# Turning feed-forward and residual blocks with VectorE block transposes and DRAM transfers

## The chip, the cores and the metric

The kernel runs on one core of one Trainium2 chip. The core has TensorE (PE in the profile; PEld are its weight loads), VectorE (DVE), ScalarE (ACT), GpSimd (POOL) and SyncE (SP), each with its own queue of instructions that run in order, a memory of 128 partitions that all engines read and write (SBUF), an accumulator memory that TensorE writes (PSUM), and DRAM, reached by transfers that SP, ACT or POOL issue. The metric is device microseconds for one execution; less is better. The time before is 2910.77 us, the median of three runs (2910.56 to 2910.94).

## The reference

Two decoder layers over 256 tokens of width 2048, and a last RMSNorm. Each layer runs a mixer (layer 0: HGRN2 and gated DeltaNet heads; layer 1: a Mamba-2 SSD mixer), a cross-attention into 256 memory tokens, and a SwiGLU feed-forward of width 5632, each behind an RMSNorm and added to the residual stream.

```python
for layer in range(DEPTH):
    u = rmsnorm(h, norm_mix[layer])
    mix = hgrn2_gdn_mixer(u, ...) if layer % 2 == 0 else mamba2_mixer(u, ...)
    h = h + mix
    xa = memory_cross_attention(rmsnorm(h, norm_xattn[layer]), rmsnorm(mem, norm_mem[layer]), ...)
    h = h + xa
    hn = rmsnorm(h, norm_ffn[layer])
    h = h + jnp.matmul(jax.nn.silu(jnp.matmul(hn, w_gate[layer])) * jnp.matmul(hn, w_up[layer]), w_down[layer])
return rmsnorm(h, norm_final)
```

All of it is in float32.

## The kernel before

**The matmuls.** All 256 tokens stay on the chip; weights are streamed from DRAM once, in tiles of 128 x 1024 floats (512 KB), four in flight (tag `wr`). A float32 weight is made into two parts of reduced width: ScalarE casts it to a high part `wh`, VectorE subtracts to get the low part `wl` (`split`, L155 to L157; four buffers each). Activations are kept in the same two parts, as operands `u` of 128 features x 4 x 256 tokens (`utiles`, L211). `xstat` (L193) computes 256 tokens x 512 columns: for each 128 rows of the weight, and for each half of the tokens, three matmuls (high by high, high by low, low by high) of 128x128 by 128x512 into a PSUM tile `acc`. So a product with 2048 rows is 16 x 2 x 3 = 96 matmuls. In it the activations are the stationary operand, so they must lie with features on the partitions.

**Where turning is needed.** `xstat` leaves tokens on the partitions. What it gives must be turned, features to the partitions, before it can be an operand again. `turned` (L282) does that on TensorE: eight transposes of 128x128 (through a matmul with the identity) for one block of 256 tokens x 512 features, into two PSUM tiles `mx`, from which ScalarE and VectorE make the two parts of the operand.

**The feed-forward** (`ffn`, L869) runs over 11 blocks of 512 hidden features in groups of 4, 4 and 3. For a block it computes the gate product, applies SiLU on ScalarE into one of the tiles `gate`, `raw` and `w`, then the up product, multiplied in by VectorE. The block is turned (`turn`, L875) one block late, behind the next block's gate product; the last block of a group is turned at the group's end. The turned blocks of a group (`hid`) are then the operand of the group's share of the down projection (`project`, L338), which adds to the residual stream `h`, four tiles `h0` to `h3` of 2 x 128 tokens x 512 features.

**The residual blocks.** A norm that follows the residual stream is a `RowNorm` (L294). As soon as a block `h[nb]` of the stream is complete, `RowNorm.block` (L304) turns it, multiplies it by the norm's gain (ScalarE makes the high part, L312; VectorE the low part, L313) and puts it on the list `u` of operands; `squares` gathers the row sums on ScalarE. There are five such norms: N1 and N2 behind the hybrid mixer and the first cross-attention, N3 behind the first feed-forward, N4 behind the SSD mixer, N5 behind the second cross-attention. N3's operands are wanted first by the SSD stage, whose first product are the step sizes (`wstat`, L172: 32 matmuls of 128x256, over all 16 rows of 128 features), and by B and C; N4's by the query projection of the second cross-attention.

**Order.** The program is written stage by stage; a planner that reckons with its own costs orders the instructions of each engine, allocates the buffers of each tag and adds the semaphores. A helper's line stands for all its uses: L121 is every matmul, L289 every transpose by `turned`, L124 and L127 VectorE's two-operand operations, L156 ScalarE's copies in `split`.

**Tags that the change uses.** `X` and `cv` (one buffer each) and `tmp` (two buffers), 4 KB per partition. Elsewhere they hold, among others, the SSD mixer's x and y of a head group (`cv`, `X`), broadcast decays (`tmp`), the queries and keys of the cross-attention (`cv`, `X`) and, in the last feed-forward's end, early parts of the down projection's weights (L357). POOL issues few transfers before the change: some scratch and row transfers of the mixers and the memory tokens.

Of the kernel before, what the change touches and what calls it, by code (L numbers as in the profile page):

```python
# [9 lines left out]
F32 = mybir.dt.float32  # L10
# [3 lines left out]
AF = mybir.ActivationFunctionType  # L14
ALU = mybir.AluOpType
# [3 lines left out]
P = 128  # L19
# [59 lines left out]
def trunk(ctx: ExitStack, tc: tile.TileContext, A: dict, out: bass.AP):  # L79
    nc = tc.nc  # L80
    pe, act, dve, pool = nc.tensor, nc.scalar, nc.vector, nc.gpsimd
# [5 lines left out]
    dp = ctx.enter_context(tc.tile_pool(name="d", bufs=1, space=bass.MemoryType.DRAM))  # L87
# [28 lines left out]
    def col(name, i=0, n=1):  # L116
        o = COLS[name][0] + i
        return cols[:, o:o + n]
# [4 lines left out]
    def tt(e, o, a, b, op):  # L123
        e.tensor_tensor(o, a, b, op=op)  # L124

    def stt(o, a, s, b, op0, op1):
        dve.scalar_tensor_tensor(o, a, s, b, op0=op0, op1=op1)  # L127

    def t4(tag, shape, dt=F32):
        return mp.tile(shape, dt, name=tag, tag=tag, bufs=BUFS.get(tag, 1))  # L130

    def psb(shape=None):
        return pm.tile(shape or [P, 512], F32, name="mx", tag="mx")
# [21 lines left out]
    def split(hi, lo, src):  # L155
        act.copy(hi, src)  # L156
        tt(dve, lo, src, hi.bitcast(F32), ALU.subtract)  # L157
# [31 lines left out]
    def later_in_stream(ins, n):  # L189

        waiting.append((len(stream) + n - 1, ins))

    def xstat(W, n0, n, u, *rows):  # L193

        accs = [pa.tile([P, n], F32, name="acc", tag="acc") for _ in range(2)]
        rows = rows or ((0, KT),)
        nk = sum(r[1] for r in rows)
        tiles = (t[1:] for r in rows for t in wtiles(W, *r, n0, n))
        for k, (wh, wl) in enumerate(tiles):
            for a in range(2):  # L200
                xh = u[k // 4][0][:, k % 4, a * P:(a + 1) * P]
                xl = u[k // 4][1][:, k % 4, a * P:(a + 1) * P]
                mm(accs[a], xh, wh, k == 0, False)
                mm(accs[a], xh, wl, False, False)
                stream.append(mm(accs[a], xl, wh, False, k == nk - 1))
                for at, ins in waiting:
                    if at == len(stream) - 1:
                        behind(ins, stream[-1])
        return accs

    def utiles():  # L211
        return (up.tile([P, 4, T], F32R, name="u", tag="u"), up.tile([P, 4, T], F32R, name="u", tag="u"))
# [41 lines left out]
    class Norm:  # L254
# [9 lines left out]
        def block(self, nb):  # L264
            src = self.load(nb)
            hi, lo = utiles()
            for c in range(4):
                g = col(self.gain[0], self.gain[1] + nb * 4 + c)
                act.activation(hi[:, c], src[:, c], AF.Copy, scale=g)
                stt(lo[:, c], src[:, c], g, hi[:, c].bitcast(F32), ALU.mult, ALU.subtract)  # L270
            self.u.append((hi, lo))
# [8 lines left out]
    h = [cp.tile([P, 2, 512], F32, name=f"h{nb}") for nb in range(4)]  # L280

    def turned(src, i, ps=None, late=0):  # L282

        if ps is None:
            ps = psb([P, 2, T])
        for x in range(2):
            c = 2 * i + x
            for a in range(2):
                ins = pe.transpose(ps[:, x, a * P:(a + 1) * P], src[a][:, c * P:(c + 1) * P], ident)  # L289
                if late:  # L290
                    later_in_stream(ins, late)
        return ps

    class RowNorm:  # L294


# [4 lines left out]
            self.ss = cp.tile([P, 2, 4], F32, name="rss", tag="rss", bufs=2)  # L301
            self.r = None

        def block(self, nb, src, late=0):  # L304
            op = utiles()
            hi, lo = op
            for i in range(2):
                ps = turned((src[:, 0], src[:, 1]), i, None, late)
                for x in range(2):
                    c = 2 * i + x  # L310
                    g = col(self.gain[0], self.gain[1] + nb * 4 + c)
                    act.activation(hi[:, c], ps[:, x], AF.Copy, scale=g)  # L312
                    stt(lo[:, c], ps[:, x], g, hi[:, c].bitcast(F32), ALU.mult, ALU.subtract)  # L313
            self.u.append(op)
            self.squares(nb, src)
# [22 lines left out]
    def project(W, u, rows, done=None, parts=None):  # L338
        for nb in range(3 if parts else 4):
            for a, acc in enumerate(xstat(W, nb * 512, 512, u, *rows)):  # L340
                hb = h[nb][:, a]
                tt(dve, hb, hb, acc, ALU.add)
                if parts:
                    parts(nb, a, 0, 512)
            if done:
                done(nb)

    def project_by_token(W, u, k0, nk, parts, done):


        t = FIRST[W[0], k0, 3 * 512, 512]
        w = []
        for i in range(nk // 2):
            raw = wp.tile([P, 2, 512], F32, name="wr", tag="wr", bufs=4)
            nc.sync.dma_start(raw, A[W[0]][W[1], t + i].rearrange("p (k n) -> p k n", n=512))
            if i < 2:
                wh, wl = (t4(tag, [P, 2, 512], F32R) for tag in (("X", "cv"), ("tmp", "tmp"))[i])  # L357
            else:
                wh, wl = (wp.tile([P, 2, 512], F32R, name=tag, tag=tag) for tag in ("wh", "wl"))
            split(wh, wl, raw)  # L360
            w.append((wh, wl))
        for a, c, n in ((0, 0, 512), (1, 0, 256), (1, 256, 256)):
            acc = pa.tile([P, n], F32, name="acc", tag="acc")
            for k in range(nk):
                wh, wl = (x[:, k % 2, c:c + n] for x in w[k // 2])
                xh, xl = (x[:, k % 4, a * P:(a + 1) * P] for x in u[k // 4])
                mm(acc, xh, wh, k == 0, False)
                mm(acc, xh, wl, False, False)
                mm(acc, xl, wh, False, k == nk - 1)
            hb = h[3][:, a, c:c + n]  # L370
            tt(dve, hb, hb, acc, ALU.add)
            parts(3, a, c, n)
            if c + n == 512:
                done(a)
# [99 lines left out]
    turns = []  # L474
# [394 lines left out]
    def ffn(layer, N, done=None, parts=None, by_token=None):  # L869
        b0 = 0  # L870
        for nblk in (4, 4, 3):
            hid = []
            late = None

            def turn(sg):  # L875
                hi, lo = op = utiles()
                for i in range(2):
                    split(hi[:, 2 * i:2 * i + 2], lo[:, 2 * i:2 * i + 2], turned(sg, i))
                hid.append(op)

            for b in range(b0, b0 + nblk):
                ga = xstat(("ffn_w_gate", layer), 512 * b, 512, N.u)
                r = N.column()
                sg = t4(("gate", "raw", "w")[b % 3], [P, 2, 512])
                sg = (sg[:, 0], sg[:, 1])
                for a in range(2):
                    act.activation(sg[a], ga[a], AF.Silu, scale=r[:, a:a + 1])
                if late:
                    turn(late)
                ua = xstat(("ffn_w_up", layer), 512 * b, 512, N.u)  # L890
                for a in range(2):
                    stt(sg[a], ua[a], r[:, a:a + 1], sg[a], ALU.mult, ALU.mult)
                late = sg
            turn(late)
            last = b0 + nblk == 11
            project(("ffn_w_down", layer), hid, ((4 * b0, 4 * nblk),), done if last else None, parts if last else None)
            if last and by_token:
                project_by_token(("ffn_w_down", layer), hid, 4 * b0, 4 * nblk, parts, by_token)
            b0 += nblk


    def ssd(N, nxt):
# [93 lines left out]
        r = ssa.column(2 * D)  # L996
        for nb in range(4):
            accs = xstat(Wo, nb * 512, 512, ys, (KT, KT))
            for a in range(2):
                p, hb = part[nb][:, a], h[nb][:, a]  # L1000
                tt(dve, p, p, accs[a], ALU.add)
                stt(hb, p, r[:, a:a + 1], hb, ALU.mult, ALU.add)
            nxt.block(nb, h[nb])


    def load_x(nb):
# [24 lines left out]
    N2 = RowNorm(("norm_ffn", 0))  # L1031
    xattn(0, N1, N2, keys)
    N3 = RowNorm(("norm_mix", 16))
    ffn(0, N2, lambda nb: N3.block(nb, h[nb]))
    N4 = RowNorm(("norm_xattn", 16))
    ssd(N3, N4)
    N5 = RowNorm(("norm_ffn", 16))
    xattn(1, N4, N5)
# [6 lines left out]
    r = cp.tile([P, 2], F32, name="r", tag="r", bufs=2)  # L1045
# [8 lines left out]
    def store(a):  # L1054
# [6 lines left out]
        for nb in range(4):  # L1061
# [5 lines left out]
            nc.sync.dma_start(out[a * P:(a + 1) * P, nb * 512:(nb + 1) * 512], hb)  # L1067

    ffn(1, N5, None, final, store)


# [49 lines left out]
```

## Time and profile before

| | us |
|---|---|
| median of the three runs | 2910.77 |
| the profiled execution | 2911.57 |
| its span, first to last instruction | 2909.8 |
| TensorE busy in it | 2891.2 |
| VectorE busy | 1770.2 |
| ScalarE busy | 1457.6 |
| GpSimd busy | 28.9 |

The granted TensorE clock is 0.998 of full speed over the span. Transfers move 542.36 MB, a mean of 186 GB/s. A busy time counts an instruction from its start to its modelled end; matmuls overlap in TensorE's pipeline, so that the sum of their durations exceeds the time that they take. What ends the program is read from the chain of work: the profile follows the last instruction back to what released it, or to the instruction before it on its engine, and gives each piece its time up to the next.

### The profile page before, as it was taken

What the parts mean: (1) busy time and instruction counts of PE and PEld (TensorE: products, weight loads), DVE (VectorE), ACT (ScalarE), POOL (GpSimd) and SP (SyncE); (2) the same over time, 40 slices, a digit from 0 to 9 for tenths busy, and PEclk for the clock granted to TensorE, in tenths of its full rate; (3) what the DMA queues carried; (4) which work ended last, traced back from release to release, by engine and by line L of the source; (5) the groups of instructions that cost most, each with busy time, mean ns of one, the idle gap of its engine ahead of it and who ended that gap; (6) DMA issues with size and microseconds to landing.
All of it is one profiled execution on the core that took longest, in us unless ns stands there. A gap on an engine that the chain in (4) does not pass through costs nothing.

```text
span 2909.8 us, 35776 instructions
## 1 busy us (share of the span) xinstructions
PE 2891.2 (99%) x13656; PEld 2402.2 (83%) x13656; DVE 1770.2 (61%) x2287; ACT 1457.6 (50%) x1834; POOL 28.9 (1%) x61
## 2 busy tenths in 40 slices
PE   8999999999999999999999999999999999999998
PEld 7888888888888888888888888888888888888887
DVE  6676768865555445445677846787664454455455
ACT  7455547655443443444655645565564443443444
POOL 0000000000000000000000000000000000000000
PEclk9999999999999999999999999999999999999999
DMA  8554544545555555555655555545555555555554
GB/s 284 173 175 141 182 145 164 191 159 188 188 188 195 188 189 192 192 189 187 206 180 195 188 198 186 188 167 182 204 185 190 189 189 194 191 190 191 195 188 153
DMA packets 154749, 542.36 MB, mean 186 GB/s; under 512 B 16968, under 2 KB 23248, under 8 KB 154576
## 3 DMA queue, kind: packets, MB, share of 16 engines
q1 hardware_dynamic: 149872, 525.11, 52.2%
q0 software_dynamic: 4288, 14.69, 1.6%
q8 instruction: 107, 1.75, 0.2%
q14 instruction: 66, 0.54, 0.1%
q10 hardware_dynamic: 416, 0.27, 0.0%
HBM read 536.13 MB, written 3.87 MB: 186 GB/s over the span
## 4 chain that ended last, share of the span: by engine, by line
PE 98%; DVE 1%; ACT 1%; issue 0%; DMA 0%; SPq 0%; DVEq 0%
PE acc L121 91%; PE mx L121 4%; PE mx L289 1%; PE tn L289 1%; PE mx L952 0%; DMA wr<-in_hy_w_in 0%; DVE wl L124 0%; ACT wh L156 0%; DVE tmp L124 0%; PE mx L489 0%; DVE b L127 0%; PE mx L601 0%; DVE X L127 0%; DVE D L124 0%; ACT D L448 0%
## 5 line engine op out<-in xcount | busy, mean ns | idle before, releaser
L121 PE MATMUL acc<-wh,u 128*128 128x512 f32 x7808 | 2445.8, 393 | 7.2 <-ACT wh L156 7.2
L124 DVE TENSOR_TENSOR wl<-wr,wh 128x1024 fp32r<-128x1024 f32 x974 | 1191.3, 1224 | 979.3 <-ACT wh L156 975.9
L121 PEld LDWEIGHTS acc<-wh,u 128*128 128x128 f32 x7808 | 1465.0, 188 | 306.3 <-ACT wh L156 7.2
L156 ACT CAST wh<-wr 128x1024 fp32r<-128x1024 f32 x978 | 1025.6, 1050 | 1210.6 <-PE acc L121 1145.1
L121 PE MATMUL acc<-wl,u 128*128 128x512 f32 x3904 | 1530.8, 392 | 1.3 <-DVE wl L124 1.3
L121 PEld LDWEIGHTS acc<-wl,u 128*128 128x128 f32 x3904 | 735.2, 188 | 151.7 <-DVE wl L124 2.7
L127 DVE SCALAR_TENSOR_TENSOR cv<-tn,cols,cv 128x255 f32<-128x255 f32 (+2 forms) x120 | 57.6, 480 | 19.3 <-ACT cv L395 17.3
L124 DVE TENSOR_TENSOR h<-h,acc 128x512 f32<-128x512 f32 (+1 forms) x89 | 57.6, 675 | 10.5 <-PE acc L121 10.3
L403 ACT ACTIVATE raw<-acc,r 128x512 f32<-128x512 f32 x64 | 42.2, 684 | 23.7 <-PE tn L289 12.0
L127 DVE SCALAR_TENSOR_TENSOR u<-mx,cols,u 128x256 fp32r<-128x256 f32 x96 | 43.2, 479 | 10.4 <-ACT u L312 6.8
L312 ACT ACTIVATE u<-mx,cols 128x256 fp32r<-128x256 f32 x80 | 34.8, 469 | 20.5 <-PE mx L289 18.1
L289 PE MATMUL tn<-cst,raw 128*128 128x128 f32 x272 | 43.7, 272 | 1.0 <-ACT raw L403 1.0
L289 PEld LDWEIGHTS tn<-cst,raw 128*128 128x128 f32 x272 | 34.1, 139 | 10.2 <-ACT raw L403 1.4
L124 DVE TENSOR_TENSOR u<-mx,u 128x512 fp32r<-128x512 f32 x48 | 31.0, 684 | 12.2 <-ACT u L156 12.2
L156 ACT CAST u<-mx 128x512 fp32r<-128x512 f32 x48 | 26.0, 591 | 16.1 <-PE mx L289 10.7
L319 ACT ACTIVATE b<-h 128x512 f32<-128x512 f32 x48 | 29.9, 624 | 1.4 <-DVE h L127 1.4
L121 PEld LDWEIGHTS mx<-tmp 128*127 128x127 f32 (+7 forms) x240 | 24.8, 178 | 1.3 <-issue 0.7
L289 PE MATMUL mx<-cst,h 128*128 128x128 f32 x160 | 25.3, 272 | 0.0
L121 PE MATMUL mx<-tmp 128*127 128x64 f32 (+7 forms) x240 | 25.0, 260 | 0.0
L127 DVE SCALAR_TENSOR_TENSOR kq<-tn,cols,kq 128x255 f32<-128x255 f32 (+2 forms) x48 | 22.8, 475 | 2.4 <-ACT kq L395 2.0
L289 PEld LDWEIGHTS mx<-cst,h 128*128 128x128 f32 x160 | 20.0, 140 | 4.9
L395 ACT ACTIVATE cv<-tn,cols 128x256 f32<-128x256 f32 x40 | 18.6, 466 | 5.2 <-PE tn L289 3.9
(281 smaller groups left out, 1129.0 us busy)
## 6 DMA issues: line engine op xcount, KB each, us to landing
wr<-in_ffn_w_gate SPq DMA_DIRECT2D x176, 512.0 KB, 3.2
wr<-in_ffn_w_up SPq DMA_DIRECT2D x176, 512.0 KB, 3.2
wr<-in_ffn_w_down SPq DMA_DIRECT2D x176, 512.0 KB, 3.2
wr<-in_ssd_w_in SPq DMA_DIRECT2D x161, 512.0 KB, 3.3
wr<-in_hy_w_in SPq DMA_DIRECT2D x129, 512.0 KB, 3.3
wr<-in_ssd_w_out SPq DMA_DIRECT2D x64, 512.0 KB, 3.3
wr<-in_hy_w_out SPq DMA_DIRECT2D x32, 512.0 KB, 4.1
tmp<-rows POOLq DMA_DIRECT2D x18, 512.0 KB, 4.1
```

What stands on the lines that cost most here:

```text
L121: return pe.matmul(o, lhsT=lhsT, rhs=rhs, start=start, stop=stop, skip_group_check=True)
L124: e.tensor_tensor(o, a, b, op=op)
L127: dve.scalar_tensor_tensor(o, a, s, b, op0=op0, op1=op1)
L156: act.copy(hi, src)
L289: ins = pe.transpose(ps[:, x, a * P:(a + 1) * P], src[a][:, c * P:(c + 1) * P], ident)
L312: act.activation(hi[:, c], ps[:, x], AF.Copy, scale=g)
L319: act.activation(t4("b2", [P, 512]), src[:, a], AF.Square, accum_out=self.ss[:, a, nb:nb + 1])
L395: act.activation(c, x, AF.Copy, scale=w[:, 3:4])
L403: act.activation(o[a], accs[a], func, scale=r[:, a:a + 1])
```

## The change

Of the blocks that are turned, some take another way. `turned_by_dma` takes the two token halves of a block (128 tokens x 512 features each). VectorE transposes each in blocks of 32x32 into a tile `y`, so that within each group of 32 partitions features and tokens have changed places. Four transfers, one for each group of 32 partitions, write `y` to a DRAM tile `turns` (two buffers), and one transfer reads it back into a tile `z` in which all 128 partitions are features. POOL issues all five. ScalarE and VectorE then make the operand's two parts from `z` in place of PSUM.

In the feed-forward (both layers) every block takes this way but the last of a group, whose operand is wanted at once. Of the residual blocks, the first three behind the first feed-forward (N3) and the first three behind the SSD mixer (N4) take it; N1, N2, N5 and each fourth block stay with TensorE. `y` and `z` lie in `X` and `cv`, or both in `tmp`, in turn. In a residual block the low part is made in eight operations of 128x128 in place of four of 128x256.

```diff
+    def turned_by_dma(src, tags):
+        y = t4(tags[0], [P, 4, 4, 2, 32])
+        z = t4(tags[1], [P, 4, 8, 32])
+        for a in range(2):
+            dve.transpose(y[:, :, :, a, :].rearrange("p b k c -> p k b c"), src[a])
+        d = dp.tile([4, 32, 4, 256], F32, name="turns", tag="turns", bufs=2)
+        for q in range(4):
+            nc.gpsimd.dma_start(d[:, :, q].rearrange("b r x -> r b x"),
+                                y[32 * q:32 * q + 32].rearrange("r b k a c -> r b (k a c)"))
+        nc.gpsimd.dma_start(z.rearrange("p q k c -> p (q k c)"), d.rearrange("b r q x -> (b r) (q x)"))
+        return z.rearrange("p q k c -> p k q c")
+
+    AWAY = (("X", "cv"), ("tmp", "tmp"))
...
-        def block(self, nb, src, late=0):
+        def block(self, nb, src, late=0, tags=None):
             op = utiles()
             hi, lo = op
-            for i in range(2):
+            if tags:
+                z = turned_by_dma((src[:, 0], src[:, 1]), tags)
+                by32 = lambda x: x.rearrange("p (a q c) -> p a q c", a=2, q=4)
+                for c in range(4):
+                    g, x = col(self.gain[0], self.gain[1] + nb * 4 + c), z[:, 2 * c:2 * c + 2]
+                    act.activation(by32(hi[:, c]), x, AF.Copy, scale=g)
+                    for a in range(2):
+                        stt(by32(lo[:, c])[:, a], x[:, a], g, by32(hi[:, c])[:, a].bitcast(F32), ALU.mult, ALU.subtract)
+            for i in range(0 if tags else 2):
                 ps = turned((src[:, 0], src[:, 1]), i, None, late)
...
-            def turn(sg):
+            def turn(sg, b):
                 hi, lo = op = utiles()
-                for i in range(2):
-                    split(hi[:, 2 * i:2 * i + 2], lo[:, 2 * i:2 * i + 2], turned(sg, i))
+                if b < b0 + nblk - 1:
+                    z = turned_by_dma(sg, AWAY[b % 2])
+                    for i in range(2):
+                        o = [x[:, 2 * i:2 * i + 2].rearrange("p k (a q c) -> p (k a) q c", a=2, q=4) for x in op]
+                        split(*o, z[:, 4 * i:4 * i + 4])
+                else:
+                    for i in range(2):
+                        split(hi[:, 2 * i:2 * i + 2], lo[:, 2 * i:2 * i + 2], turned(sg, i))
                 hid.append(op)
...
                 if late:
-                    turn(late)
+                    turn(late, b - 1)
...
-            turn(late)
+            turn(late, b)
...
-            nxt.block(nb, h[nb])
+            nxt.block(nb, h[nb], 0, AWAY[nb % 2] if nb < 3 else None)
...
-    ffn(0, N2, lambda nb: N3.block(nb, h[nb]))
+    ffn(0, N2, lambda nb: N3.block(nb, h[nb], 0, AWAY[nb % 2] if nb < 3 else None))
```

## The prediction

> **What bounds the kernel now.** I read the page's busy times first, then its chain of work that ended last, then what TensorE waited for, and then the chain in order of time where the removed work stands.
>
> ```profile
> PE 2891.2 (99%) x13656; PEld 2402.2 (83%) x13656; DVE 1770.2 (61%) x2287; ACT 1457.6 (50%) x1834; POOL 28.9 (1%) x61
> ...
> PE 98%; DVE 1%; ACT 1%; issue 0%; DMA 0%; SPq 0%; DVEq 0%
> ```
> ```profile
> PE acc L121 <- ACT wh L156: 7.2, 1, 7.2
> PE acc L121 <- DVE wl L124: 1.3, 2, 0.9
> PE tn L289 <- ACT raw L403: 1.0, 1, 1.0
> PE mx L121 <- ACT MD L856: 0.6, 2, 0.3
> ```
> ```profile
> ACT wh L156 <- PE acc L121: 1145.1, 702, 5.0
> DVE wl L124 <- ACT wh L156: 975.9, 762, 3.5
> ```
>
> TensorE (PE) is the chain for 98% of the span. All that it ever waited for comes to 10.1 us, 7.2 of it a single wait. ScalarE (ACT) waits 1145 us, in 702 pieces, for TensorE to free a weight buffer, and VectorE (DVE) waits behind ScalarE. So work taken off TensorE shortens the span one for one, until ScalarE, VectorE or a transfer is late instead.
>
> A busy time is not a price here: matmuls overlap in the pipeline. The price is read from the chain, where a piece ends as the next starts. The first three rows are a middle turn of the first feed-forward, the next five the first residual block behind that feed-forward.
>
> ```profile
> 1037.01 0.87 PE mx L289 x8
> 1037.88 43.55 PE acc L121 x192
> 1081.43 0.87 PE mx L289 x8
> ```
> ```profile
> 1346.50 0.22 PE mx L289 x2
> 1346.72 0.23 PE acc L121
> 1346.95 0.66 PE mx L289 x6
> 1347.60 16.14 PE acc L121 x71
> 1363.74 0.22 PE mx L289 x2
> ```
> Eight transposes take 0.87 us, 0.109 us each, and a matmul takes 43.55 / 192 = 0.227 us. A period of the residual blocks is 1363.74 - 1346.50 = 17.24 us with 72 matmuls; 72 x 0.227 = 16.33, so a block costs 0.91 us; I take the same for those behind the SSD mixer.
>
> **What is removed.**
>
> ```profile
> L289 PE MATMUL mx<-cst,h x160: 270/273/273, 566.6 to 2178.5; 128*128 128x128 f32 x160
> L289 PE MATMUL mx<-cst,gate x64: 269/273/273, 727.6 to 2812.6; 128*128 128x128 f32 x64
> L289 PE MATMUL mx<-cst,raw x64: 270/273/273, 772.1 to 2840.3; 128*128 128x128 f32 x64
> L289 PE MATMUL mx<-cst,w x48: 271/273/273, 816.5 to 2768.2; 128*128 128x128 f32 x48
> ```
>
> Gate, raw and w are the feed-forward tiles: 176 transposes, 22 blocks of 8. Each layer's groups of 4, 4 and 3 blocks keep the last block on TensorE, so 3 + 3 + 2 = 8 blocks go per layer, 16 in all. Of the 20 residual blocks (160 / 8), three go behind the first feed-forward and three behind the SSD mixer. That is 22 blocks, 176 transposes: 16 x 0.87 + 6 x 0.91 = 13.9 + 5.5 = **19.4 us** off the chain. (Durations would say 176 x 0.273 = 48 us; that counts the pipeline's overlap.)
>
> **What is added.** Each block now takes two block transposes of 128x512 on VectorE, four writes and one read on the POOL queue, and the same splitting into high and low part, from SBUF. No duration of the new shapes is in the trace; the nearest rows follow.
>
> ```profile
> L638 DVE STREAM_TRANSPOSE XT<-X x4: 695/706/712, 172.2 to 331.2; 128x512 f32<-128x512 f32 x4
> ```
> ```profile
> L127 DVE SCALAR_TENSOR_TENSOR u<-mx,cols,u 128x256 fp32r<-128x256 f32 x96 | 43.2, 479 | 10.4 <-ACT u L312 6.8 <-ACT u L498 3.4
> L124 DVE TENSOR_TENSOR u<-mx,u 128x512 fp32r<-128x512 f32 x48 | 31.0, 684 | 12.2 <-ACT u L156 12.2
> L127 DVE SCALAR_TENSOR_TENSOR b<-mx,hms,gate 128x128 f32<-128x128 f32 x24 | 6.5, 344 | 0.1
> ```
> ```profile
> wr<-in_ffn_w_gate SPq DMA_DIRECT2D x176, 512.0 KB, 3.2
> ...
> tmp<-rows POOLq DMA_DIRECT2D x18, 512.0 KB, 4.1
> scratch<-MD POOLq DMA_DIRECT2D x4, 256.0 KB, 3.1
> X<-scratch POOLq DMA_DIRECT2D x4, 256.0 KB, 5.6
> scratch<-b POOLq DMA_DIRECT2D x2, 256.0 KB, 5.0
> ```
> ```profile
> 134.28 0.75 POOL L618 DMA_DIRECT2D scratch<-MD  x1 [74.97 <-DVE MD L127]
> 166.18 1.50 POOL L635 DMA_DIRECT2D X<-scratch  x2 [1.86 <-DMA scratch<-b]
> ```
>
> VectorE gains 44 x 0.706 = 31 us, and 6 x (8 x 0.344 - 4 x 0.479) = 5 us since a residual block's low part is now made in eight halves: 36 us on 1770, at 61% busy. ScalarE's count and sizes stay. POOL gains 110 issues of 0.75, 83 us on an engine that is 1% busy. Transfers gain 22 x 1 MB (128 x 1024 floats, written and read), 4% of what the kernel moves now:
>
> ```profile
> DMA packets 154749, 542.36 MB, mean 186 GB/s; under 512 B 16968, under 2 KB 23248, under 8 KB 154576
> ```
>
> None of these sums is near a bound; what matters is when the turned block arrives.
>
> The path of one block: transposes 1.4 us; four issues, the last starting 2.25 behind the first and landing 3.1 later (5.0 by the slowest write row), 5.4 (7.3); the read 5.6 (4.1 by the fastest row); the split 2.0, or 2.75 for a residual block. That is 14.4 us (12.9 to 16.3) in the feed-forward and 15.2 us (13.7 to 17.1) for a residual block. Up to two weight splits of 1.23 us may stand ahead on VectorE: 2.5 more. I take the middle.
>
> When it is wanted: in the feed-forward not before the down projection, where the second-last block of a group is the third operand of four (the second of three). It lies a whole gate and up pass behind its source, 43.5 us (the 43.55 us piece above); with the transposes issued only at the old place, still the up half, some 22 us. So 14 to 19 us hide there. Behind the SSD mixer the next block's 96 matmuls cover 96 x 0.227 = 21.8 us. Behind the first feed-forward it is tight:
>
> ```profile
> 1375.82 1.28 DVE L124 TENSOR_TENSOR h<-h,acc 128x512 f32<-128x512 f32 x2
> ...
> 1393.31 3.04 PE L121 MATMUL acc<-u,wh 128*128 128x256 f32 x24
> ```
>
> The third residual block is complete at 1377.1. The 24 matmuls at 1393.31 are the step sizes' first three quarters; theirs of the third block start 16 x 3.04 / 24 = 2.0 us in, at 1395.3, and 0.9 us earlier without a turn in between: 17.3 us for a path of 15.2 (13.7 to 19.6 with the splits). Stall: nothing to 2.3 us, once. I take 0.5.
>
> **A wait is added**: ScalarE's and VectorE's splits now wait for a transfer, and behind them on the same queues stand the weight splits for which TensorE waits. What they have in hand:
>
> ```profile
> 831.21 1.05 ACT L156 CAST wh<-wr 128x1024 fp32r<-128x1024 f32 x1 [1.67 <-PE acc L121]
> 832.29 1.23 DVE L124 TENSOR_TENSOR wl<-wr,wh 128x1024 fp32r<-128x1024 f32 x1 [1.50 <-ACT wh L156]
> 833.93 1.05 ACT L156 CAST wh<-wr 128x1024 fp32r<-128x1024 f32 x1 [1.67 <-PE acc L121]
> ```
> ```profile
> 329.42 0.71 DVE L638 STREAM_TRANSPOSE XT<-X 128x512 f32<-128x512 f32 x1 [5.66 <-DMA X<-scratch]
> ```
>
> A tile lasts TensorE 2.72 us (833.93 - 831.21) and there are four; a buffer just freed is due in 3 x 2.72 = 8.2 us and takes 1.05 + 1.23 to fill, so some 6 us of standing still cost nothing. The last row bears it out: VectorE stood 5.66 us for a transfer of just this kind, and no wait of TensorE above reaches 1 us on VectorE. I cost the wait at nothing, and at what exceeds 6 us if the planner puts the splits too early.
>
> A rule that speaks against the change: the Trainium skill, "SBUF — State Buffer", section "SBUF: two separate sides", says that descriptors for transfers issued by GpSimd are written by GpSimd itself through a port shared with VectorE, which VectorE holds in two-port modes (or, against GpSimd reads, with two SBUF inputs). With one weight split of 1.23 us ahead of each of five issues, an estimate by that rule is 6 us more per block. The trace does not show it: the two issues at 166.18 took 0.75 us each in a stretch in which VectorE (the third figure behind the span) was busy 14.24 of 20 us.
>
> ```profile
> 160.00:180.00 20.00, 20.00 (x98) 16.75 (x97) 14.24 (x25) 12.09 (x15) 3.05 (x6) 1.00 0.73 239
> ```
>
> **Sum.** The profiled execution took 2911.57 us, its span 2909.8. 2911.57 - 19.4 + 0.5 = 2892.7. It ran 0.8 us above the median of the runs, 2910.77, so the median comes to **2892 us**, -0.6%.
>
> **Rivals.**
> - *Late at the border behind the first feed-forward.* For: only some 2 us in hand, and a path that no row shows whole. Against: one place, three blocks, and TensorE has gate matmuls to go on with, as it has now. If each issue also waits for one weight split of 1.23 us on VectorE, 5 x 1.23 = 6.2 us are added to the 2.3: 2892 to 2900; were the paths longer still by 4 us, 2904. 18%. (The page on SBUF named above would give such waits a cause.)
> - *Slower: the splits block their queues.* If the planner reckons a transfer far too short, ScalarE or VectorE stands in front of the unlanded read. From 6 us of standing TensorE starves, and from 6 + 0.87 us a block loses more than it saves. If the wait is the read and the write before it, 5.6 + 0.75 + 3.1 = 9.5 us, each block costs 3.5: 22 x 3.5 = 77 us, 2968 us; a stand of 7.5 us gives 2911 - 19 + 33 = 2925. For: these engines take instructions in order, and one such stand of 5.66 us is on record. Against: it was harmless, and of the waits on POOL transfers by these engines it is the longest. 7%.
> - *No change: the time freed is not passed on,* since 1 MB per block delays the weight loads or another engine becomes the bound. A weight load lands in 3.2 us (the first of the transfer rows above) and may take four tiles' time, 10.9 us; VectorE and ScalarE have 1770 and 1458 us of 2892. 2905 to 2911. 5%.
> - *More than reckoned,* from another order that the planner finds in the stages behind (it orders by its own costs; the waits of 10.1 us bound most of this): 2885 to 2889. 4%.
>
> **How the numbers follow.** The forecast holds 66% (2889 to 2895), the late border 18%, blocked queues 7%, no change 5%, more 4%. 2888 to 2904 takes in the first two and part of the last, with at most 2 in 10 left out. About 0.2%, 5.8 us, is what a measurement of this kernel can tell from no change. Faster by over that (below 2904.9): 66 + 17 + 4 = 87%; within it 7%; slower 6%, being most of the blocked queues.
>
> **What would show it.** In the profile after: 336 - 176 = 160 of these four groups of transposes left (112 from h, 48 from the feed-forward tiles); in the chain the 0.87 us pieces gone from between gate and up except ahead of a down projection; 110 POOL issues more and 44 block transposes near 0.7 us. TensorE's waits should stay near 10 us. The forecast is wrong if ScalarE or VectorE shows waits on the read above 6 us followed by a wait of TensorE on wh or wl, if TensorE waits on u where the SSD stage begins, or if weight loads land far later than 3.2 us.

## The result, and the profile after

The changed kernel took 2894.22 us in the median of six runs (2889.94 to 2898.10), the kernel before 2910.77 (six runs, 2907.08 to 2911.05): 16.6 us less, a ratio of 0.9947 with a 95% interval of [0.9937, 0.9958]. The forecast was 2892.0 in a range of 2888 to 2904. The profiled execution took 2893.56 us, its span 2891.8.

First the page's busy times and chain of the changed kernel, then what TensorE waited for in it.

```profile
PE 2872.3 (99%) x13480; PEld 2383.0 (82%) x13480; DVE 1794.3 (62%) x2355; ACT 1455.2 (50%) x1834; POOL 89.8 (3%) x171
...
PE 97%; DVE 1%; DMA 1%; ACT 1%; issue 0%; POOL 0%; DVEq 0%; SPq 0%; POOLq 0%
```
```profile
PE acc L121 <- ACT wh L156: 6.6, 1, 6.6
PE acc L121 <- DVE wl L124: 2.8, 2, 1.9
PE tn L289 <- ACT raw L427: 1.0, 1, 1.0
PE mx L121 <- ACT MD L880: 0.6, 2, 0.3
```

TensorE has exactly 176 matmuls fewer (13656 - 13480), POOL 110 issues more. The chain is still TensorE's; the share of transfers in it went from 0% to 1%. Of TensorE's waits three are about as they were; the wait on the low part of a weight has one piece of 1.9 us that was not there, and lost one of 0.4 us that the kernel before has in the SSD mixer, at 1666 us.

Where that piece lies is seen from the chain in order of time. Each row below starts at the same instruction in both kernels: behind the last transposes ahead of the first feed-forward, of the first feed-forward, in the SSD mixer's last group but one, in the second cross-attention, and behind the last transposes of the second feed-forward. The first fence is the kernel before, the second the changed one; columns are start, time, engine and line.

```profile
668.59 59.22 PE acc L121 x261
...
1330.36 16.14 PE acc L121 x71
...
1940.93 3.38 PE mx L121 x34
...
2147.09 10.91 PE acc L121 x48
...
2840.59 60.81 PE acc L121 x302
```
```profile
667.40 172.77 PE acc L121 x762
...
1321.84 8.67 PE acc L121 x38
...
1933.02 3.38 PE mx L121 x34
...
2136.41 10.92 PE acc L121 x48
...
2822.58 60.81 PE acc L121 x302
```

The differences between neighbouring rows are the stages. In the feed-forwards they repeat between executions to a hundredth of a microsecond, in the other stages to some tenths where nothing waits (the table of the experiments below has them), so they show what the medians can't:

| stage, us | before | changed | difference |
|---|---|---|---|
| up to the first feed-forward (nothing changed) | 668.59 | 667.40 | -1.19 |
| first feed-forward, 8 blocks | 661.77 | 654.44 | -7.33 |
| border (N3, 3 blocks) and SSD mixer | 610.57 | 611.18 | +0.61 |
| N4 (3 blocks), second cross-attention | 206.16 | 203.39 | -2.77 |
| second feed-forward, 8 blocks | 693.50 | 686.17 | -7.33 |

In the feed-forward's chain, 172.77 us run without a break where three turns stood before. The four stages that the change touches come to -16.82. The border alone gave nothing: three blocks should have paid 2.8 us there, as they did behind the SSD mixer, and it is 0.6 us longer.

ScalarE's waits for the reads in the changed kernel (in total, times, longest):

```profile
ACT u L156 <- DMA cv<-turns: 44.9, 10, 5.3
ACT u L156 <- DMA tmp<-turns: 26.7, 6, 5.0
ACT u L328 <- DMA cv<-turns: 12.9, 4, 4.0
ACT u L328 <- DMA tmp<-turns: 5.9, 1, 5.9
```

So it stood in front of an unlanded read in 21 of 22 blocks, 4.5 us on average in the 16 feed-forward blocks ((44.9 + 26.7) / 16). There TensorE did not wait once. At the border it did. ScalarE, VectorE and TensorE there, from the timeline of each:

```profile
1363.68 1.05 ACT L156 CAST wh<-wr 128x1024 fp32r<-128x1024 f32 x1 [2.17 <-DMA wr<-in_ffn_w_down]
1370.67 1.71 ACT L328 ACTIVATE u<-tmp,cols 128x256 fp32r<-128x256 f32 x4 [5.94 <-DMA tmp<-turns]
1372.29 1.03 ACT L156 CAST wh<-wr 128x1024 fp32r<-128x1024 f32 x1
```
```profile
1371.21 0.61 DVE L127 SCALAR_TENSOR_TENSOR u<-tmp,cols,u 128x128 fp32r<-128x128 f32 x2 [5.22 <-ACT u L328]
1371.74 0.68 DVE L124 TENSOR_TENSOR h<-h,acc 128x512 f32<-128x512 f32 x1
1372.34 0.61 DVE L127 SCALAR_TENSOR_TENSOR u<-tmp,cols,u 128x128 fp32r<-128x128 f32 x2
1372.87 0.68 DVE L124 TENSOR_TENSOR h<-h,acc 128x512 f32<-128x512 f32 x1
1373.46 1.13 DVE L127 SCALAR_TENSOR_TENSOR u<-tmp,cols,u 128x128 fp32r<-128x128 f32 x4
1374.51 0.70 DVE L300 STREAM_TRANSPOSE X<-h 128x512 f32<-128x512 f32 x1
1375.14 1.18 DVE L124 TENSOR_TENSOR wl<-wr,wh 128x1024 fp32r<-128x1024 f32 x1
```
```profile
1376.38 0.50 PE L121 MATMUL acc<-wl,u 128*128 128x512 f32 x1 [1.91 <-DVE wl L124]
```

ScalarE stood 5.94 us for the second block's read, and its next weight cast began only at 1372.29. VectorE stood 5.22 us behind it and then had 3.9 us of other work (1371.21 to 1375.14: the low part in eight halves, two additions to the residual stream, the third block's first transpose) ahead of the weight's low part. The cast was done at 1373.32 (1372.29 + 1.03), and the low part began 1.8 us later: nearly the whole of TensorE's wait of 1.91 us is VectorE's other work, met behind the stand. TensorE ran out. And it paid twice. The next view gives stretches of time: length, busy time of PE, PEld, DVE, ACT and POOL (each with its count), then the granted clock, the DMA share and GB/s.

```profile
1374.00:1376.00 2.00, 0.47 (x3) 0.04 (x1) 2.00 (x5) 2.00 (x4) 0.00 (x0) 1.00 0.00 0
1376.00:1378.00 2.00, 1.62 (x5) 1.30 (x6) 2.00 (x4) 0.96 (x2) 0.76 (x2) 0.69 0.34 63
1378.00:1380.00 2.00, 2.00 (x6) 1.61 (x5) 1.78 (x3) 0.00 (x0) 1.42 (x3) 0.50 0.95 289
1380.00:1384.00 4.00, 4.00 (x18) 3.24 (x17) 0.69 (x1) 1.31 (x2) 0.00 (x0) 0.98 0.93 319
```

0.31 x 2 + 0.50 x 2 + 0.02 x 4 = 1.7 us are lost to the lower clock after 1.9 us of waiting: 3.6 us together. The gap between the three blocks' pay and the border's +0.61 is 3.4, or 3.8 with the 0.4 us of the wait in the SSD mixer that is gone.

### The profile page after: what moved, and what is told of

It is laid out like the page before. It is cut to its first block, busy times and chain, and to the rows that moved or that the text cites. A ratio compares the mean times of both kernels' runs of the same rounds, so it can differ in the third digit from the quotient of the medians.

```text
span 2891.8 us, 35717 instructions
## 1 busy us (share of the span) xinstructions
PE 2872.3 (99%) x13480; PEld 2383.0 (82%) x13480; DVE 1794.3 (62%) x2355; ACT 1455.2 (50%) x1834; POOL 89.8 (3%) x171
## 4 chain that ended last, share of the span: by engine, by line
PE 97%; DVE 1%; DMA 1%; ACT 1%; issue 0%; POOL 0%; DVEq 0%; SPq 0%; POOLq 0%
PE acc L121 90%; PE mx L121 4%; PE tn L289 1%; PE mx L289 1%; DVE wl L124 0%; PE mx L982 0%; DMA turns<-X 0%; DMA tmp<-turns 0%; DMA turns<-tmp 0%; DMA cv<-turns 0%; ACT wh L156 0%; DMA wr<-in_hy_w_in 0%; DVE h L124 0%; DVE u L127 0%; DVE tmp L124 0%
## 5 line engine op out<-in xcount | busy, mean ns | idle before, releaser
L124 DVE TENSOR_TENSOR wl<-wr,wh 128x1024 fp32r<-128x1024 f32 x974 | 1186.2, 1222 | 858.8 <-ACT wh L156 855.5
L303 POOL DMA_DIRECT2D turns<-X x56 | 30.6, 554 | 1389.0 <-DVE X L300 1389.0
L127 DVE SCALAR_TENSOR_TENSOR cv<-tn,cols,cv 128x255 f32<-128x255 f32 (+2 forms) x120 | 57.5, 479 | 17.7 <-ACT cv L419 15.6
L124 DVE TENSOR_TENSOR u<-cv,u 128x512 fp32r<-128x512 f32 x20 | 12.9, 688 | 38.8 <-ACT u L156 38.8
L127 DVE SCALAR_TENSOR_TENSOR u<-mx,cols,u 128x256 fp32r<-128x256 f32 x72 | 32.6, 478 | 5.1 <-ACT u L522 2.6
L156 ACT CAST u<-cv 128x512 fp32r<-128x512 f32 x20 | 11.4, 618 | 44.9 <-DMA cv<-turns 44.9
L336 ACT ACTIVATE u<-mx,cols 128x256 fp32r<-128x256 f32 x56 | 24.6, 468 | 11.7 <-PE mx L289 9.4
L303 POOL DMA_DIRECT2D turns<-tmp x32 | 17.5, 553 | 228.3 <-DVE tmp L300 227.0
L465 POOL DMA_DIRECT2D tmp<-rows x18 | 10.1, 563 | 463.6 <-DVE D L124 442.0
```

The source lines that it names most:

```text
L303: nc.gpsimd.dma_start(d[:, :, q].rearrange("b r x -> r b x"), y[32 * q:32 * q + 32].rearrange("r b k a c -> r b (k a c)"))
L465: nc.gpsimd.dma_start(R, gr[h0:h0 + 4].partition_broadcast(P))
```

## The experiments

The theory (A in the expectations): TensorE time is saved one for one in all 22 blocks, and at the border it is given back because ScalarE stands in front of the read and blocks the weight splits behind it. The rival (B): the transfers slow the weight loads all over, which also makes the changed kernel's runs lie 8 us apart. The last column of this table is the sum of the four changed stages against the kernel before in the profiled executions; where a median is given, the kernel before, measured beside it, had 2910.77 (changed), 2908.47 (no_n3 to only_n3), 2910.22 (three_before to all_turned) and 2908.67 (the last two).

| kernel | median, us | ratio, 95% interval | first ff | border, SSD | N4, attention | second ff | sum |
|---|---|---|---|---|---|---|---|
| changed | 2894.22 | 0.9947 [0.9937, 0.9958] | -7.33 | +0.61 | -2.77 | -7.33 | -16.8 |
| no_n3 | 2890.84 | 0.9946 [0.9933, 0.9960] | -7.33 | +0.01 | -2.77 | -7.33 | -17.4 |
| held | 2890.53 | 0.9939 [0.9927, 0.9952] | -7.34 | -3.21 | -2.75 | -7.33 | -20.6 |
| no_trip | 2890.23 | 0.9935 [0.9923, 0.9947] | -7.33 | -2.76 | -2.78 | -7.33 | -20.2 |
| only_n3 | 2911.96 | 1.0009 [1.0000, 1.0018] | -0.01 | +2.22 | 0.00 | -0.01 | +2.2 |
| three_before | 2933.25 | 1.0081 [1.0064, 1.0098] | +0.78 | +9.93 | +1.34 | +0.75 | +12.8 |
| three_after | 2938.45 | 1.0099 [1.0084, 1.0114] | -1.08 | +18.96 | +2.69 | -3.19 | +17.4 |
| all_turned | 2904.28 | 0.9980 [0.9970, 0.9989] | | | | | |
| after_again | 2891.64 | 0.9943 [0.9930, 0.9956] | -7.33 | +1.88 | -2.27 | -7.34 | -15.1 |
| held_again | 2890.49 | 0.9933 [0.9919, 0.9947] | -7.33 | -3.08 | -2.68 | -7.34 | -20.4 |

**no_n3: the border's blocks back on TensorE.**

```diff
-    ffn(0, N2, lambda nb: N3.block(nb, h[nb], 0, AWAY[nb % 2] if nb < 3 else None))
+    ffn(0, N2, lambda nb: N3.block(nb, h[nb]))
```

> The three residual blocks behind the first feed-forward (N3) go back to TensorE; the 16 feed-forward blocks and the three behind the SSD mixer (N4) keep the transfers. Theory A (the change pays 0.9 us of TensorE per block everywhere, and at the N3 border ScalarE standing in front of the read starves TensorE and the clock drops behind it): 14.7 us from the feed-forwards and 2.8 from N4, 2893.3 us, and the runs lie within some 1 us of one another; no wait of TensorE near the border. Theory B (transfers delay the weight loads everywhere, which makes the spread of 8 us between the runs of the changed kernel): 2893 to 2898, spread as before the edit.

The border's stage is back at what it was before to 0.01 us, and the wait on the low part is as it was:

```profile
PE acc L121 <- DVE wl L124: 1.3, 2, 0.9
```

But the runs lie 6.3 us apart (2889.63 to 2895.98), so the part of theory A about the spread fell, and with it B's: the kernel before, in 15 runs on this chip, lies 5 us apart itself, eight runs at 2906.4 to 2908.5 and seven at 2909.5 to 2911.5.

**held: the splits of the turned blocks later on ScalarE's queue.** Nothing else is changed in what is computed; the splits of all but the third block at the border and the third behind the SSD mixer are ordered behind a later weight cast.

```diff
+    def hold(ins, n):
+        held.append((len(casts) + n, ins))
...
-                        split(*o, z[:, 4 * i:4 * i + 4])
+                        split(*o, z[:, 4 * i:4 * i + 4], 1)
...
-                    act.activation(by32(hi[:, c]), x, AF.Copy, scale=g)
+                    ins = act.activation(by32(hi[:, c]), x, AF.Copy, scale=g)
+                    if n is not None:
+                        hold(ins, n)
...
+            for at, x in held:
+                if at == len(casts):
+                    behind(x, ins)
```

> All 22 blocks by transfers, but the reading halves of the split are held on ScalarE's queue behind a later weight cast: behind the second cast of the up half in the feed-forward, behind the tenth cast at the first two N3 blocks and the eleventh at the first two N4 blocks. Theory A: ScalarE's waits on the read shrink from 90 us in sum to under 25, TensorE no longer waits at the border, 2911 less 20.1 = 2890.7 us, spread about 1 us. Theory B: the transfers are the same, so 2894 with the same spread of several us.

ScalarE's waits for the reads fall from 90.4 us to the first row below, what is left at three residual blocks: the third of either place, which were not held, and the first behind the SSD mixer, not held long enough; TensorE's wait on the low part to the second.

```profile
ACT u L340 <- DMA cv<-turns: 9.7, 3, 4.0
```
```profile
PE acc L121 <- DVE wl L124: 0.9, 1, 0.9
```

The chain runs through the border without a break (the first row starts behind the last transposes of the first feed-forward, the second where the stage ends):

```profile
1321.63 64.83 PE acc L121 x297
...
1928.99 3.38 PE mx L121 x34
```

The border's stage pays 3.21 us with the same transfers: the price of its three blocks, 2.8, and the 0.4 us of the wait in the SSD mixer, which is gone here as it is in the changed kernel (why was not tried). The median was 2890.53 where 2890.7 was expected; the spread, again, was not 1 but 4.5 us.

**no_trip: the transfers left out.** The split reads the block-transposed tile itself, so that the turned features are out of order.

```diff
-        d = dp.tile([4, 32, 4, 256], F32, name="turns", tag="turns", bufs=2)
-        for q in range(4):
-            nc.gpsimd.dma_start(d[:, :, q].rearrange("b r x -> r b x"),
-                                y[32 * q:32 * q + 32].rearrange("r b k a c -> r b (k a c)"))
-        nc.gpsimd.dma_start(z.rearrange("p q k c -> p (q k c)"), d.rearrange("b r q x -> (b r) (q x)"))
+        z = y.rearrange("p b k a c -> p (b k a c)").rearrange("p (q k c) -> p q k c", q=4, k=8)
```

> The five transfers of each block are left out: the split reads VectorE's block-transposed tile itself, so the features of the turned blocks are out of order in the result. Theory A: nothing to stand for, 2890.7 us as with held splits, spread about 1 us, weight loads back at 3.2 us. Theory B: also 2890.7; if held splits give 2894 and this 2890.7, the transfers' load is the cost; if both give 2890.7, the standing is.

With no transfer to wait for, every block pays its 0.92 us: 20.2 in sum. That held splits with all transfers reach the same says that the 23 MB of transfers cost nothing where nothing stands in front of them. It also bears on the two parts of the border's loss: VectorE's own work there is still in this kernel, and without the stand it costs nothing. The stand without that work was not tried. Two expectations failed: the runs lie 4.1 us apart, not 1, and the weight loads did not come back to 3.2 us.

```profile
wr<-in_ffn_w_gate SPq DMA_DIRECT2D x176, 512.0 KB, 4.4
```

They land in 4.4 us without a single added transfer (4.3 in the changed kernel), in only_n3 in 3.3. So it is not the transfers that make them longer; what does is open, and it costs nothing here.

**only_n3: the border's blocks alone by transfers.** The feed-forward and N4 stay on TensorE.

```diff
-                if b < b0 + nblk - 1:
+                if False:
...
-            nxt.block(nb, h[nb], 0, AWAY[nb % 2] if nb < 3 else None)
+            nxt.block(nb, h[nb])
```

> Only the three N3 blocks go by transfers. Theory A: 2.7 us saved on TensorE, 2 to 6 us given back at the border: 2909 to 2914 us, and it alone shows the spread between runs; TensorE waits about 2 us on the low part of a weight near 1390 us. Theory B: 2908.1 us, spread within 1 us, since only three blocks load the transfers.

Its median lies 3.5 us above the kernel before, its border's stage 2.2 us above, with the two feed-forwards and the attention as they were. The spread of its runs, 5.9 us, is not its own, as the kernel before and the other kernels with four buffers have 4 to 9 us too. What TensorE waited for near the border, from its timeline:

```profile
1382.66 0.73 PE L121 MATMUL acc<-wh,u 128*128 128x512 f32 x2 [0.35 <-ACT wh L156]
...
1385.67 0.79 PE L121 MATMUL acc<-wl,u 128*128 128x512 f32 x1 [2.28 <-DVE wl L124]
...
1400.80 0.39 PE L121 MATMUL acc<-u,wh 128*128 128x256 f32 x1 [0.36 <-ACT u L328]
```

The main wait is the blocked queue again. The third block being late for the step sizes, which the prediction had feared, is there too, with 0.36 us.

**three_before, three_after: three weight buffers in place of four,** in the kernel before and in the changed one.

```diff
-    wp = ctx.enter_context(tc.tile_pool(name="w", bufs=4))
+    wp = ctx.enter_context(tc.tile_pool(name="w", bufs=3))
```

> The kernel before with three weight buffers (raw tiles still four) in place of four. Queue theory: a weight split may then come 3.4 us late (2 x 2.72 less 1.05 and 1.23, and the low part is due 0.23 later) in place of 6.1 before TensorE waits; without the transfers nothing in the feed-forward is as late as that, so the time stays within 3 us of the kernel before. Rival (the cushion is not what hides the standing): also unchanged.

> The changed kernel with three weight buffers. In the feed-forward a weight cast now comes 4.05 us late (due at 718.49, done standing and splitting at 722.54). Queue theory: above 3.4 us, so each of the 16 feed-forward blocks makes TensorE wait 0.5 to 2 us, with a lower clock for some us behind it (1.5 us lost): the gain of 17 us is eaten up, 2895 to 2930 us, and waits of TensorE on wl appear inside the feed-forwards. Rival (standing is free whatever the buffers): same gain as with four, 17 us below the three-buffer kernel before.

The first expectation was wrong: the kernel before loses 23 us already. That loss is not in the feed-forward, where TensorE never idles (first row; the second figure is its busy time). Its largest part, 9.9 us, lies in the stage of the border and the SSD mixer (second row, 7.4 us of idle), 5.9 lie ahead of everything that the change touches. With the change, TensorE idles in the first feed-forward too (second fence, 2.9 us).

```profile
668.00:1330.00 662.00, 662.00 (x2964) 547.45 (x2963) 332.76 (x316) 280.49 (x294) 0.00 (x0) 1.00 0.57 190
...
1400.00:2000.00 600.00, 592.60 (x2866) 483.56 (x2865) 425.26 (x560) 345.99 (x446) 9.54 (x17) 1.00 0.56 187
```
```profile
668.00:1330.00 662.00, 659.09 (x2908) 542.21 (x2907) 342.87 (x334) 280.10 (x295) 21.96 (x40) 1.00 0.62 203
```

Measured from row to row of the chain as above, the first feed-forward takes 662.55 us in three_before and 660.69 in three_after: 1.9 us saved in place of 7.3; the second saves 3.9. TensorE's waits on weights there are shorter than expected (0.53 us at most) and come to 4.0 us in the two. The largest loss is again at the border: with the SSD mixer it takes 9.0 us more than in three_before, and N4 with the attention 1.4 more. So the time came out above the 2895 to 2930 that was expected, both because three buffers cost 23 us by themselves and because of the border. Over all, the change makes the kernel 5.2 us slower with three buffers where it makes it 17 faster with four. The same standing in the feed-forward that is free with four buffers in hand is paid in part with three.

**all_turned: the last block of each group by transfers too,** on top of the held splits; the splits of these last blocks are not held.

```diff
-                if b < b0 + nblk - 1:
+                if True:
```

> As the kernel with held splits, and the last block of each feed-forward group goes by transfers too (28 blocks). Its operand is wanted 16.3 us behind its source in a group of four (12 x 6 x 0.227) and 10.9 in a group of three; the path took some 16 us. Slack theory: 0 to 2 us of waiting for u in the groups of four, some 5 us and a lower clock behind it in the groups of three, against 0.92 us saved each: 2893 to 2905 us, slower than with held splits (2890.5). Rival (TensorE's saved time is what counts wherever the block is): 2885 us.

13.8 us slower than held splits by the medians, for six blocks; 1.8 of it is how far the kernel before lay apart on the two occasions. TensorE's new wait:

```profile
PE acc L121 <- ACT u L161: 13.2, 6, 3.6
```

It waits for the operand itself, up to 3.6 us. So the last block of a group has too little in hand for this path, as the arithmetic of when it is wanted said.

**after_again, held_again: the changed kernel and held splits side by side,** unchanged from above.

> The changed kernel as it is, beside the one with held splits on the same chip. The stages say 16.8 us below the kernel before; a wait of TensorE of some 2 us on a weight's low part near 1376 us, and the clock granted at half for some 3 us behind it.

> The kernel with held splits once more, beside the changed kernel. The stages say 20.6 us below the kernel before and 3.8 below the changed kernel, with no wait of TensorE at the border. If the border is not the cause, both lie within 1 us.

The wait expected in the changed kernel is there: 2.17 us on a weight's low part, ended at 1377.28. By the stages the held version is 5.3 us better (20.4 against 15.1), all but 0.4 of it at the border. By the medians it is 1.2 us better here, and over all runs on both occasions the means are 2893.2 (11 runs of the changed kernel) and 2889.7 (10 runs of the held one). Held splits are the fastest kernel of this study that computes the whole reference; the intervals of the two ratios overlap, so the order of the two rests on the stages and on the wait that is gone, not on the medians.

## Why the prediction was right or wrong

The time was forecast at 2892.0 and came at 2894.2, for the reason that was given: TensorE was the chain, and what was taken off it came back as time. That the number came so near is in part luck: the sum took 0.8 us too little for what is removed and 2.9 too little for the stall, two errors that partly cancel, and 1.2 us of the profiled execution's gain lie ahead of everything that was changed.

- **What is removed**, 0.87 us for a feed-forward block, 0.91 for a residual one, 19.4 in sum. The stages say 7.33 / 8 = 0.92 for both kinds, 20.2 in sum (no_trip, where nothing interferes). The chain's piece of 0.87 was some hundredths short of what a turn costs.
- **What is added** beside it. The block transposes took 0.70 us (0.706 taken), VectorE gained 24 us in sum (36 reckoned), the POOL issues 0.55 us each (0.75 taken). The path of the first border block, from the transpose's start at 1333.96 to the last low part at 1351.66, took 17.7 us. The prediction had 15.2, 13.7 to 17.1, and up to 2.5 more for weight splits in between, so it lies within the bounds but not at the value taken. The rows of the trace:

```profile
1335.55 2.18 POOL L303 DMA_DIRECT2D turns<-X  x4 [51.89 <-DVE X L300]
1343.98 0.56 POOL L305 DMA_DIRECT2D cv<-turns  x1 [6.25 <-DMA turns<-X]
```

  POOL stood 6.25 us behind its last issue for the writes to land, against 3.1 taken and 5.0 as the upper row; the median of the changed kernel's 88 writes of 128 KB is 4.5 us from issue to landing.
- **The added wait, "I cost the wait at nothing, and at what exceeds 6 us".** Right for the 16 feed-forward blocks (4.5 us of standing on average), for N4 (3.40 and 3.99 us; its second block did not stand) and for the first border block (3.74 us): no loss. Right in its condition too: with three buffers the standing in the feed-forward costs. **This step failed at the second block of the border.** The 6 us in hand were reckoned for a queue that has only weight splits behind the wait. There the stand of 5.94 us met a VectorE queue with 3.9 us of other work ahead of the weight split, and the two add up to more than is in hand. (They exceed 6 us by 3.9, and TensorE waited 1.9, so the sum says where a wait comes, not how long it is.)
- **"Stall: nothing to 2.3 us, once. I take 0.5."** The place was right, the mechanism wrong. The prediction let the third block's operand be late for the step sizes. What was late is the weight, behind the second block's read; the late operand shows only in two other executions (0.36 and 0.5 us). The term measured 3.4 us by the stages, 3.6 in the trace: 1.9 of waiting and about 1.7 of lower clock, which the prediction did not reckon with at all.
- **The rule on the shared port** gave no rival a price in the end: the 88 writes' issues took 551 to 576 ns, although VectorE spends 41% of the span on the weights' two-input splits alone (1186.2 us). The Trainium skill ("SBUF — State Buffer", "SBUF: two separate sides") would have the later of the two block, for an instruction with two SBUF inputs only against a GpSimd instruction that reads SBUF; no issue here shows it. The prediction's 6 us took the weight splits to hold back the writing of descriptors, which that condition does not say. Whether the writes' 6.25 us holds a part of such a wait was not tried.
- **The range and the rivals.** 2894.2 lies in the forecast's own 2889 to 2895 and in the late border's 2892 to 2904. The border was late, but by the mechanism of the blocked queues, at one block; no change and slower by blocked queues everywhere did not come. The sign of being wrong, a stand above 6 us and a wait of TensorE behind it, was all but there: 5.94 and 1.91 us. Weight loads landed in 4.3 us in place of 3.2, at no cost that the stages show.

## What to carry to other kernels

Work taken off the engine that is the chain pays its in-stream spacing (0.11 us per transpose), not its listed duration (0.27), and does so wherever its replacement lands in time. By these runs a wait for a transfer on an engine that also feeds the chain is free only up to the buffers in hand, less all other work queued between the wait and the feeding instruction; count that work at each place by itself. Where it is not free, keep the transfer and move the waiting instruction later on its queue: that gave back all of the 3.8 us between the changed kernel's border and the held one's.

## What the runs showed of the hardware

- After 1.9 us without a matmul TensorE's clock fell to 0.50 (1378 to 1380 us), and the 1.7 us lost are worth some 3.4 us at that clock, so a short wait cost nearly double. Behind the waits of 2.17 us (after_again) and 2.28 (only_n3) at the same place it fell likewise, to 0.61 over 1378 to 1382 and 0.66 over 1386 to 1390; in held, no_trip and no_n3, with no wait there, it stayed at 1.00, and in all_turned it did so behind a wait of 0.97 us at 849. The Trainium skill ("TensorE: Matmul & The Clock Gate", "Why this matters for your kernels") puts the danger at idle gaps above about 3 us; here a shorter one was enough.
- The clock also dropped far from any such wait: in the profile of the kernel before, between 256 and 260 us, within the hybrid mixer, TensorE is busy all the time and the granted clock is 0.50. Its last wait, 0.98 us, had ended at 245.40.

```profile
252.00:256.00 4.00, 4.00 (x37) 3.93 (x35) 2.85 (x4) 3.85 (x6) 0.00 (x0) 0.96 0.69 239
256.00:260.00 4.00, 4.00 (x13) 3.33 (x13) 2.02 (x11) 2.92 (x5) 0.00 (x0) 0.50 0.34 121
260.00:264.00 4.00, 4.00 (x16) 3.15 (x15) 2.54 (x9) 1.04 (x1) 0.00 (x0) 0.68 0.00 0
```

  In the profiles of no_n3 and held_again no such drop shows, though a wait of 1.0 us stands there too, and they reach the first feed-forward at 664.5 and 664.6 us in place of 668.6. These 4 us would fit the two groups in which the runs of the kernel before lie, but the clock granted over each run bears that out in 11 of the 15 only. The drop stands ahead of everything that the change touches; what decides whether it comes was not tried.
